# One-pass gate product, operands fetched ahead, and a re-ordered recurrence in a GLA + RWKV-7 block

## The chip, the cores and the metric

One Trainium2 chip, of which the kernel uses one core. The metric is the device time of one execution in microseconds (us), as the median of several runs. TensorE (PE) multiplies matrices from SBUF into PSUM; VectorE (DVE), ScalarE (ACT) and GpSimd (POOL) work on elements; SyncE (SP) issues the DMAs. Each engine runs its own instruction list in order and waits on semaphores that others raise.

## The reference, cut to what matters

x has 2048 rows of 1024. A row-normalised h = RMSNorm(x) is multiplied by a wide matrix; the columns feed a GLA branch, an RWKV-7 branch and two gates.

```python
p = h @ w_in                                     # GLA | RWKV-7 | merge gates
# GLA: chunked gated linear attention, forward and backward, 4 heads
la_f = log_sigmoid(af @ wa2_f + ba_f) / 16       # the gate product: af has 16 columns
la_b = log_sigmoid(ab @ wa2_b + ba_b) / 16
y_a  = (norm(gla(q, k, v, la_f) + flip(gla(flip ..., la_b))) * silu(og)) @ gla_proj
# RWKV-7: s = token shift of p; decay and a from low-rank products
w = decay(w0 + tanh(wl) @ w2); a = sigmoid(a0 + al @ a2); g = sigmoid(gl) @ g2
S_t = S_{t-1} diag(w_t) + (S_{t-1} a_t) b_t^T + v_t k_t^T;  y_t = S_t r_t   # both directions, 8 heads
y_b = (groupnorm(y) + sum(r * k * r_k) * v) * g @ rwkv_proj
x = x + (sigmoid(gA) * y_a + sigmoid(gB) * y_b) @ w_out
x = x + convglu(rmsnorm(x)); out = rmsnorm(x)
```

## The kernel before, in words

Large products are made of three passes: each operand is split into hi (rounded to float32r) and lo (the rest), and hi·hi, hi·lo and lo·hi are summed in one PSUM bank (`mm3`, L237). The stages, with their times in the profiled execution:

* **0 to 275 us**: RMSNorm, the v columns, the low-rank columns af (L393 to L406: PSUM rows 0 to 31 hold the product with the weights' hi, rows 32 to 63 that with their lo; both go to DRAM scratch d_af) and the first projections.
* **275 to 620 us, GLA**: `gla()` is a generator that is stepped beside the projections (`Weave`, L590). For each of 4 heads and 4 blocks of 512 tokens, `gla_gate` (L486) multiplies wa2 (64 rows, float32) with af into z, from which the decays follow.
* **620 to 1045 us, RWKV preparation**: `rwkv_prep(p, b)` (L725) for 4 head pairs and 4 blocks, beside the remaining projections. It loads twal (tanh of wl, and al), shifts k, r and v, makes three low-rank products from twal (L741, L747), the scans, the operands arbk that go to d_lt, the transposes of v (L799), and the bonus product from sr (L805, L807). Each `yield` hands over to the projections.
* **1045 to 1893 us, recurrence**: 32 chunks of 64 steps, both directions d side by side. For a chunk, `sc_mm` (L864) loads the operands Lt and makes the score blocks psc, seven chunks ahead (LA); `sc_ev` (L877) masks them on DVE into Q (L880) and in place (L881), then ACT copies parts of Q into Nb (L887) and the rest over Lt (L889). Every four chunks `invert` (L917) turns Nb into the triangular inverses TT. The chain from chunk to chunk is W (L990), U (L1014), S (L1025) and X (L1027); py and Y are the output.
* In the same loop `fill()` (L1127) spreads the gate projections (kind g, 36 units of 6 steps) and the GLA output projection (kind y, 32 units of 3 steps) over the chunks, two steps of four products at four places of a chunk. Its helpers `w_get` (load a weight into the single buffer wraw), `w_put` (split it into whi and wlo, two buffers each), `o_get`, `o_put`, `g_get` and `g_sig` are laid on fixed steps (L1164 to L1202): a weight is put two steps before its first use, and the next is fetched right after. All its loads and stores go through SP, and the operands, gates and results share three buffers ev.
* **From 1893 us** the merge, the output projection and the MLP, not touched.

Order: up to the recurrence a planner orders each engine's list by a simulated timeline and priorities. Inside the loop over chunks (L1283) the lists of PE, ACT, DVE and POOL stand in the order of the program (`manual_schedule`); SP's is still the planner's. PSUM and SBUF tiles rotate over the number of buffers that `bufs` gives, and a new tile waits for the last reader of the one that it replaces.

Of the kernel before, what the change touches and what calls it, by code (L numbers as in the profile page):

```python
# [23 lines left out]
NB = 4  # L24
# [80 lines left out]
def _pack(inputs):  # L105
# [9 lines left out]
    wa = np.zeros((64, 4, 128), np.float32)  # L115
    f, b = one("gla_wa2_f"), one("gla_wa2_b")
    for h in range(4):
        for r0 in (0, 32):
            wa[r0:r0 + 16, h, :64] = f[:, h * 64:h * 64 + 64]
            wa[r0 + 16:r0 + 32, h, 64:] = b[:, h * 64:h * 64 + 64]  # L120
# [46 lines left out]
def _body(tc, A, out, dump=None, upto=99):  # L167
# [12 lines left out]
    def scratch(name, shape):  # L180
        return dr.tile(shape, F32, name=name, tag=name)
# [3 lines left out]
    d_af = scratch("d_af", [64, T])  # L185
# [213 lines left out]
    for b in range(NB):  # L399
# [4 lines left out]
        o = ev.tile([128, 512], F32, name="ev", tag="ev")  # L404
        nc.scalar.copy(out=o[0:64, :], in_=ps[0:64, :])
        sync.dma_start(out=d_af[:, b * BT:(b + 1) * BT], in_=o[0:64, :])  # L406
# [17 lines left out]
    wa2 = gp.tile([64, 4, 128], F32, name="wa2")  # L424
    sync.dma_start(out=wa2, in_=A["wa2"])
# [43 lines left out]
    def gla_load(hs, b):  # L469
# [5 lines left out]
        af = gp.tile([64, 512], F32, name="af", tag="af", bufs=1)  # L475
        sync.dma_start(out=af, in_=d_af[:, ts])
# [247 lines left out]

    def rwkv_prep(p, b):  # L725
# [3 lines left out]
        twal = R["rp"].tile([128, 512], F32, name="twal", tag="twal")  # L729
        sync.dma_start(out=twal, in_=d_twal[:, ts])  # L730
# [3 lines left out]
        if b == 0:  # L734
            R["lora"] = R["rp"].tile([128, 2, 128], F32, name="lora", tag="lora")
            sync.dma_start(out=R["lora"], in_=A["lora"][:, :, pc])
# [17 lines left out]
        yield  # L754

# [39 lines left out]
        nc.scalar.copy(out=tmp, in_=sv[:, ::-1])  # L795
        for d, sx in enumerate((sv, tmp)):
# [8 lines left out]
        nc.vector.scalar_tensor_tensor(out=sr, in0=sr, scalar=vc("rk", p), in1=kp, op0=ALU.mult, op1=ALU.mult)  # L805
# [39 lines left out]
    NL = 2 * LA + 1  # L845
# [12 lines left out]
    qs = {}  # L858
# [5 lines left out]
    def sc_mm(s, d):  # L864
        Lt = cl.tile([128, 2, 4, 128], F32, name="Lt", tag="Lt", bufs=NL)
        sync.dma_start(out=Lt, in_=d_lt[d, :, chunk_of(s, d)])
        Q = cl.tile([128, 4, 128], F32, name="Q", tag="Q", bufs=NL)
# [9 lines left out]
    def sc_ev(c):  # L877
# [39 lines left out]
    def invert(n):  # L917
        X = cp.tile([128, 32, 32], F32, name="XX", tag="XX", bufs=2)
# [364 lines left out]
    with tc.manual_schedule(engines=ORDERED):  # L1283
        for s in range(32):
# [4 lines left out]
            if not last:  # L1289
                scale_bj(s + 1, 1, bjs[1])  # L1290
# [544 lines left out]
```

## Time and profile before

| | |
|---|---|
| time, median of 3 runs | 3528.93 us (3526.49 to 3532.44) |
| profiled execution: time, span | 3531.8 us, 3530.0 us |
| mean granted TensorE clock (share of 2.4 GHz) | 0.961 |
| PE / PE weight loads busy | 93% / 74% |
| DVE / ACT / POOL busy | 65% / 46% / 25% |
| DMA | 531 MB, 151 GB/s on the mean |

The span runs from the first to the last instruction. A group of rows further down is one view of the trace: busy time by stretch, waits by who waited for whom, or instructions in order of time. "A <- B" in a wait means that A's engine stood idle until B had ended. Matmuls are pipelined: the step from one to the next is the start of the next less its own start, shorter than its duration.

### The profile page before, as it was taken

How to read it: one execution, taken by the hardware profiler on the slowest of the kernel's cores; microseconds unless marked ns; L12 is line 12 of the kernel's file. 1: busy time of each engine (PE TensorE's matmuls, PEld its weight loads, DVE VectorE, ACT ScalarE, POOL GpSimd, SP SyncE). 2: the span in 40 equal slices, each digit the busy share in tenths (PEclk: the TensorE clock that was granted, in tenths of full speed). 3: DMA queues.
4: the chain of work that ended last, by engine and by line, in shares of the span. 5: the costliest groups of instructions: out<-in, count | busy, mean ns of one | idle time of the engine just before them, and what ended most of it. 6: DMA issues, size and time to landing. Idle time of an engine off the chain costs nothing.

```text
span 3530.0 us, 58016 instructions
## 1 busy us (share of the span) xinstructions
PE 3282.4 (93%) x22232; PEld 2626.9 (74%) x22232; DVE 2281.4 (65%) x3903; ACT 1609.0 (46%) x2912; POOL 875.7 (25%) x715
## 2 busy tenths in 40 slices
PE   7999999999988888887777999999999999999999
PEld 6787778766656777766666788888877888878887
DVE  5207664587865666666776566888989989623222
ACT  4214443455545776776644333544454444411111
POOL 1122222134440000000002411666665555000000
PEclk9999999999999998998888999999999999999999
DMA  4233343687875455556788846422242222523222
GB/s 150 94 117 108 127 141 122 187 227 224 232 214 180 150 183 157 171 184 195 229 254 282 294 142 191 134 81 89 79 136 96 84 84 78 182 82 112 80 85 63
DMA packets 403222, 531.29 MB, mean 151 GB/s; under 512 B 61504, under 2 KB 250560, under 8 KB 402944
## 3 DMA queue, kind: packets, MB, share of 16 engines
q1 hardware_dynamic: 402944, 527.58, 48.0%
q8 instruction: 175, 2.87, 0.3%
q14 instruction: 103, 0.84, 0.1%
HBM read 345.02 MB, written 181.93 MB: 149 GB/s over the span
## 4 chain that ended last, share of the span: by engine, by line
PE 48%; DVE 12%; DMA 6%; ACT 4%; issue 2%; SPq 1%; POOL 0%; DVEq 0%; ACTq 0%; POOLq 0%
PE pu L1638 20%; PE pg L241 6%; PE pd L1722 4%; PE pd L1724 4%; PE pd L1723 4%; PE pf L1218 3%; DVE tm L924 1%; DVE XX L925 1%; DMA d_m<-ev 1%; DMA wraw<-win 1%; DVE X L1027 1%; DVE gX L1004 1%; DVE wlo L227 1%; ACT TT L938 1%; DMA ev<-d_gate 1%
## 5 line engine op out<-in xcount | busy, mean ns | idle before, releaser
L227 POOL TENSOR_TENSOR wlo<-wraw,whi 128x1024 fp32r<-128x1024 f32 x46 | 115.3, 2507 | 1175.0 <-ACT whi L226 929.1
L1561 POOL TENSOR_TENSOR rw<-rw 128x512 f32<-128x512 f32 x168 | 282.1, 1694 | 72.4 <-DVE s3l L227 59.7
L1722 PE MATMUL pd<-wdh,whi 128*128 128x512 f32 x672 | 261.6, 391 | 0.9 <-DVE ug L1506 0.9
L1723 PE MATMUL pd<-wdl,whi 128*128 128x512 f32 x672 | 261.4, 389 | 0.0
L1724 PE MATMUL pd<-wdh,wlo 128*128 128x512 f32 x672 | 259.3, 389 | 0.0
L1218 PE MATMUL pf<-fop,whi 128*128 128x512 f32 x576 | 178.6, 448 | 85.3 <-ACT whi L226 58.3
L241 PE MATMUL pg<-hlo,whi 128*128 128x512 f32 x928 | 254.2, 407 | 0.0
L241 PE MATMUL pg<-hhi,whi 128*128 128x512 f32 x928 | 249.7, 404 | 3.1 <-ACT whi L226 3.1
L241 PE MATMUL pg<-hhi,wlo 128*128 128x512 f32 x928 | 248.2, 402 | 0.0
L241 PEld LDWEIGHTS pg<-hhi,whi 128*128 128x128 f32 x928 | 176.2, 192 | 55.9 <-issue 15.8
L241 PEld LDWEIGHTS pg<-hlo,whi 128*128 128x128 f32 x928 | 176.9, 194 | 53.9 <-issue 18.1
L241 PEld LDWEIGHTS pg<-hhi,wlo 128*128 128x128 f32 x928 | 176.1, 192 | 50.6 <-issue 14.3
L1218 PEld LDWEIGHTS pf<-fop,whi 128*128 128x128 f32 x576 | 114.1, 209 | 122.1 <-ACT whi L226 64.1
L226 ACT CAST whi<-wraw 128x1024 fp32r<-128x1024 f32 x114 | 119.5, 1048 | 112.9 <-PE pg L241 54.1
L1606 DVE SCALAR_TENSOR_TENSOR cv<-ug,vec,cv 128x511 f32<-128x511 f32 (+1 forms) x88 | 124.1, 1410 | 57.4 <-ACT cv L1605 57.4
L1711 ACT CAST whi<-wraw 128x1024 fp32r<-128x1024 f32 (+1 forms) x36 | 35.3, 980 | 267.1 <-PE pd L1723 186.6
L1722 PEld LDWEIGHTS pd<-wdh,whi 128*128 128x128 f32 x672 | 126.1, 188 | 29.9 <-issue 4.2
L1724 PEld LDWEIGHTS pd<-wdh,wlo 128*128 128x128 f32 x672 | 126.1, 188 | 26.2
L1723 PEld LDWEIGHTS pd<-wdl,whi 128*128 128x128 f32 x672 | 126.1, 188 | 25.7
L1613 ACT ACTIVATE cv<-cv 128x511 f32<-128x511 f32 (+1 forms) x84 | 53.3, 634 | 197.0 <-DVE cv L1607 197.0
L1714 DVE TENSOR_TENSOR wlo<-wraw,whi 128x1024 fp32r<-128x1024 f32 (+1 forms) x36 | 39.3, 1091 | 151.4 <-ACT whi L1711 151.4
L227 DVE TENSOR_TENSOR wlo<-wraw,whi 128x1024 fp32r<-128x1024 f32 x68 | 84.1, 1237 | 79.3 <-ACT whi L226 79.2
(482 smaller groups left out, 8119.9 us busy)
## 6 DMA issues: line engine op xcount, KB each, us to landing
rw<-wup SPq DMA_DIRECT2D x84, 512.0 KB, 3.5
wraw<-win SPq DMA_DIRECT2D x74, 512.0 KB, 4.3
Lt<-d_lt SPq DMA_DIRECT2D x64, 512.0 KB, 5.2
d_lt<-arbk SPq DMA_DIRECT2D x96, 256.0 KB, 3.9
d_gate<-ev SPq DMA_DIRECT2D x64, 256.0 KB, 3.7
X<-d_vt SPq DMA_DIRECT2D x64, 256.0 KB, 4.4
bj<-d_lt SPq DMA_DIRECT2D x128, 128.0 KB, 3.8
d_m<-ev SPq DMA_DIRECT2D x64, 256.0 KB, 5.3
```

The lines of the kernel that those rows point to most:

```text
L226: (hi_eng or nc.scalar.copy)(out=hi, in_=src)
L227: (lo_eng or nc.vector).tensor_tensor(out=lo, in0=src, in1=hi.bitcast(F32), op=ALU.subtract)
L241: nc.tensor.matmul(ps, (wh, wh, wl)[ph], (xh, xl, xh)[ph], start=(ph == 0 and i == 0), stop=(ph == 2 and i == n - 1))
L1218: nc.tensor.matmul(ps, (wh, wh, wl)[ph][:, k0 + k, :], (hi, lo, hi)[ph][:, k, :], start=i == first[u] and k == 0, stop=i == last[u] and k ...
L1561: ps_ = lambda o, x, y, op: nc.gpsimd.tensor_tensor(out=o, in0=x, in1=y, op=op)
L1606: nc.vector.scalar_tensor_tensor(out=c, in0=u[:, c0 - 1:c0 - 1 + n], scalar=vc("cw0", m), in1=c, op0=ALU.mult, op1=ALU.add)
L1613: nc.scalar.activation(out=g, in_=g, func=AF.Silu)
L1638: nc.tensor.matmul(ps, w_, x_, start=first and n == 0, stop=n == len(mm) - 1, skip_group_check=True)
L1714: nc.vector.tensor_tensor(out=al[:, 0:m], in0=raw[:, 0:m], in1=ah[:, 0:m].bitcast(F32), op=ALU.subtract)
L1722: nc.tensor.matmul(ps, a, wdh[k][:, cs], start=(k == 0), stop=False)
L1723: nc.tensor.matmul(ps, a, wdl[k][:, cs], start=False, stop=False)
L1724: nc.tensor.matmul(ps, l, wdh[k][:, cs], start=False, stop=False)
```

## The change

* *Gate product.* d_af gets 128 rows: hi and lo of the first product, hi of the second, and hi of the first again. wa2 gets 128 rows of float32r, hi in rows 0 to 95 and lo in rows 96 to 127. One float32r product per block and head takes the place of the float32 one.
* *Preparation.* `get_low` loads twal (and at the start of a head pair the low-rank weights) right after the three products of the block before. sr is scaled by r_k and k before the transposes of v, not after.
* *Scores.* The two directions' Q share one tile, with 8 buffers in place of 15 single ones; Lt has 14 buffers (15 before). `sc_ev` is cut in two: `sc_v` (the DVE part) stays, `sc_a` (the ACT part) comes later: that of direction 0 before the scores of direction 1, that of direction 1 in the next chunk behind scale_bj, unless an inversion starts. The copies into Nb take both directions at once.
* *Fill.* A weight is put five steps ahead of its first use, the first one already before the prologue; all loads and stores of the fill are issued by GpSimd.

```diff
-    wa = np.zeros((64, 4, 128), np.float32)
+    wa = np.zeros((128, 4, 128), np.float32)
-        for r0 in (0, 32):
+        for r0 in (0, 32, 64, 96):
...
-        o = ev.tile([128, 512], F32, name="ev", tag="ev")
+        o = ev.tile([128, 512], F32R, name="ev", tag="ev")
+        ol = ev.tile([128, 512], F32R, name="ev", tag="ev")
         nc.scalar.copy(out=o[0:64, :], in_=ps[0:64, :])
-        sync.dma_start(out=d_af[:, b * BT:(b + 1) * BT], in_=o[0:64, :])
+        nc.vector.tensor_tensor(out=ol[0:32, :], in0=ps[0:32, :], in1=o[0:32, :].bitcast(F32), op=ALU.subtract)
+        for r0, src in ((0, o[0:32]), (32, ol[0:32]), (64, o[32:64]), (96, o[0:32])):
+            sync.dma_start(out=d_af[r0:r0 + 32, b * BT:(b + 1) * BT], in_=src.bitcast(F32))
...
-    wa2 = gp.tile([64, 4, 128], F32, name="wa2")
-    sync.dma_start(out=wa2, in_=A["wa2"])
+    wa2 = gp.tile([128, 4, 128], F32R, name="wa2")
+    war = ev.tile([128, 4, 128], F32, name="ev", tag="ev")
+    sync.dma_start(out=war, in_=A["wa2"])
+    nc.scalar.copy(out=wa2, in_=war)
+    nc.vector.tensor_tensor(out=wa2[96:128], in0=war[96:128], in1=wa2[96:128].bitcast(F32), op=ALU.subtract)
...
-        af = gp.tile([64, 512], F32, name="af", tag="af", bufs=1)
+        af = gp.tile([128, 512], F32R, name="af", tag="af", bufs=1)
...
+    def get_low(p, b):
+        R["twal"] = R["rp"].tile([128, 512], F32, name="twal", tag="twal")
+        sync.dma_start(out=R["twal"], in_=d_twal[:, b * BT:(b + 1) * BT])
+        if b == 0:
+            R["lora"] = R["rp"].tile([128, 2, 128], F32, name="lora", tag="lora")
+            sync.dma_start(out=R["lora"], in_=A["lora"][:, :, p * 128:p * 128 + 128])
...
-        twal = R["rp"].tile([128, 512], F32, name="twal", tag="twal")
-        sync.dma_start(out=twal, in_=d_twal[:, ts])
+        if (p, b) == (0, 0):
+            get_low(0, 0)
+        twal = R["twal"]
...
         act_tail[0] = last
         yield
+        if (p, b) != (3, NB - 1):
+            get_low(p + (b + 1) // NB, (b + 1) % NB)
...
         nc.scalar.copy(out=tmp, in_=sv[:, ::-1])
+        nc.vector.scalar_tensor_tensor(out=sr, in0=sr, scalar=vc("rk", p), in1=kp, op0=ALU.mult, op1=ALU.mult)
         for d, sx in enumerate((sv, tmp)):
...
         yield
-        nc.vector.scalar_tensor_tensor(out=sr, in0=sr, scalar=vc("rk", p), in1=kp, op0=ALU.mult, op1=ALU.mult)
         pn = R["rs"].tile([128, 512], F32, name="pn", tag="pn", bufs=2)
...
-    NL = 2 * LA + 1
+    NL = 2 * LA
...
-        Q = cl.tile([128, 4, 128], F32, name="Q", tag="Q", bufs=NL)
+        if d == 0:
+            qg[s] = cl.tile([128, 2, 4, 128], F32, name="Q", tag="Q", bufs=LA + 1)
+        Q = qg[s][:, d]
...
-    def sc_ev(c):
+    def sc_v(c):
         s, d, Lt, Q, ps = c
         mb_ = mk[d].unsqueeze(1).to_broadcast([128, 4, 128])
         nc.vector.tensor_tensor(out=Q, in0=ps[0], in1=mb_, op=ALU.mult)
         nc.vector.tensor_tensor(out=ps[1], in0=ps[1], in1=mb_, op=ALU.mult)
-        if d == 0 and s % 4 == 0:
-            nbs[s // 4] = cp.tile([128, 8, 4, 32], F32, name="Nb", tag="Nb")
-        for q in range(4):
-            rr = slice(q * 32, q * 32 + 32)
-            c0 = (q % 2) * 32
-            nc.scalar.copy(out=nbs[s // 4][rr, (s % 4) * 2 + d], in_=Q[rr, :, c0:c0 + 32])
+
+    def sc_a(c):
+        if c is None:
+            return
+        s, d, Lt, Q, ps = c
+        if d:
+            if s % 4 == 0:
+                nbs[s // 4] = cp.tile([128, 8, 4, 32], F32, name="Nb", tag="Nb")
+            for q in range(4):
+                rr = slice(q * 32, q * 32 + 32)
+                c0 = (q % 2) * 32
+                nc.scalar.copy(out=nbs[s // 4][rr, (s % 4) * 2:(s % 4) * 2 + 2], in_=qg[s][rr, :, :, c0:c0 + 32])
         for e in range(2):
             nc.scalar.copy(out=Lt[EV[e], 1 - e], in_=ps[1][EV[e]])
...
             raw = wp.tile([128, 1024], F32, name="wraw", tag="wraw", bufs=1)
-            sync.dma_start(out=raw, in_=A["win"][units[u][1]] if units[u][0] == "g" else A["wpa"][units[u][1] // 2])
+            nc.gpsimd.dma_start(out=raw, in_=A["win"][units[u][1]] if units[u][0] == "g" else A["wpa"][units[u][1] // 2])
...
-        puts = [max(first[u] - 2, done_[wid[fresh[i - 2]]] + 1 if i > 1 else 0) for i, u in enumerate(fresh)]
+        puts = [max(first[u] - 5, done_[wid[fresh[i - 2]]] + 1 if i > 1 else 0) for i, u in enumerate(fresh)]
         for i, u in enumerate(fresh):
             if i:
                 at(puts[i - 1], w_get, u)
-            at(puts[i], w_put, u)
+                at(puts[i], w_put, u)
...
         w_get(0)
+        w_put(0)
         yield
...
+    fil(1)
     load_x(0)
...
         for s in range(32):
...
             if not last:
                 scale_bj(s + 1, 1, bjs[1])
+            sc_a(c1)
...
+            c0 = c1 = None
             if la < 32:
-                c = sc_mm(la, 0)
-                sc_ev(c)
+                c0 = sc_mm(la, 0)
+                sc_v(c0)
...
+            sc_a(c0)
             if la < 32:
-                c = sc_mm(la, 1)
-                sc_ev(c)
+                c1 = sc_mm(la, 1)
+                sc_v(c1)
             if fresh:
+                sc_a(c1)
+                c1 = None
                 sl.add(invert(s // 4 + 1))
```

The four other DMAs of the fill (o_get, g_get, and the stores of d_gate and d_m) change from `sync` to `nc.gpsimd` like w_get's; in the prologue sc_a follows sc_v at once; gn_out takes one Q pair for its two tiles.

## Rows read from the trace of the kernel before

**Rows 1.** The page's busy time by engine: us, share of the span, instructions.

```profile
PE 3282.4 (93%) x22232; PEld 2626.9 (74%) x22232; DVE 2281.4 (65%) x3903; ACT 1609.0 (46%) x2912; POOL 875.7 (25%) x715
```

**Rows 2.** Busy time by stretch; the columns are named in the first line.

```profile
core 0: us, PE busy (x) PEld busy (x) DVE busy (x) ACT busy (x) POOL busy (x), PEclk, DMA share, GB/s
275.00:620.00 345.00, 343.40 (x1819) 272.28 (x1819) 224.34 (x575) 146.01 (x353) 83.46 (x69) 1.00 0.40 127
620.00:1045.00 425.00, 393.49 (x1496) 277.55 (x1495) 325.96 (x420) 232.37 (x353) 164.85 (x116) 0.94 0.76 215
1045.00:1165.00 120.00, 96.87 (x1112) 77.58 (x1113) 58.60 (x113) 66.37 (x145) 5.74 (x9) 0.89 0.58 178
1165.00:1690.00 525.00, 445.34 (x7926) 367.93 (x7925) 345.88 (x660) 370.00 (x804) 0.00 (x0) 0.92 0.57 177
1690.00:1893.00 203.00, 148.43 (x1742) 118.71 (x1734) 158.84 (x336) 106.82 (x225) 2.46 (x1) 0.83 0.82 235
```

**Rows 3.** Waits of PE, 1165 to 1690: us in total, times, longest.

```profile
PE pf L1218 <- ACT whi L226: 44.0, 11, 6.7
PE pf L1218 <- ACT fop L226: 11.9, 3, 6.2
```

**Rows 4.** Waits of ACT, same stretch.

```profile
ACT Nb L887 <- DVE Q L880: 77.0, 46, 5.4
```

**Rows 5.** Waits of SP's queue, same stretch.

```profile
SPq L1154 <- DVE wlo L227: 43.3, 10, 7.8
```

**Rows 6.** Instructions in time, PE, 277 to 281: start, us, what.

```profile
278.10 1.12 PE L491 MATMUL z<-af,wa 64*128 64x512 f32 x2
279.15 1.19 PE L241 MATMUL pg<-hhi,whi 128*128 128x512 f32 x4
```

**Rows 7.** Waits of PE, 620 to 1045.

```profile
PE pw L741 <- DMA twal<-d_twal: 17.9, 9, 3.2
PE pn L807 <- DVE sr L805: 5.0, 6, 1.2
```

**Rows 8.** Waits of PE, 1045 to 1165.

```profile
PE pf L1218 <- ACT whi L226: 12.9, 3, 8.8
```

**Rows 9.** Groups by line, ACT, 1045 to 1893: busy us, mean ns, idle.

```profile
L887 ACT COPY Nb<-Q 32x128 f32<-32x128 f32 x256 | 75.6, 295 | 80.2 <-DVE Q L880 77.8
```

**Rows 10.** Busy time by stretch: an undisturbed chunk, and 24 chunks.

```profile
1236.50:1252.30 15.80, 15.80 (x265) 13.29 (x264) 7.46 (x12) 9.93 (x24) 0.00 (x0) 1.00 0.60 185
1173.10:1699.30 526.20, 444.93 (x7875) 367.15 (x7874) 346.80 (x665) 369.99 (x803) 0.00 (x0) 0.92 0.57 178
```

**Rows 11.** Instructions in time, 1235.9 to 1243.

```profile
1236.62 0.34 SPq L1154 DMA_DIRECT2D wraw<-win  x1
...
1237.50 1.10 PE L997 MATMUL py<-X,Lt 128*64 128x64 f32 x32
...
1238.17 0.86 SPq L866 DMA_DIRECT2D Lt<-d_lt  x2
...
1241.89 0.33 PE L874 MATMUL psc<-Lt 64*64 64x128 f32 x2
```

**Rows 12.** The page's DMA issues: count, KB each, median us to landing.

```profile
rw<-wup SPq DMA_DIRECT2D x84, 512.0 KB, 3.5
...
Lt<-d_lt SPq DMA_DIRECT2D x64, 512.0 KB, 5.2
...
d_m<-ev SPq DMA_DIRECT2D x64, 256.0 KB, 5.3
```

**Rows 13.** Waits of PE, 1690 to 1893.

```profile
PE pf L1218 <- ACT whi L226: 24.0, 5, 10.0
```

**Rows 14.** Chain that ended last by line, 1690 to 1893.

```profile
by line: DMA d_m<-ev 15.5%; DMA ev<-d_gate 10.3%; PE pf L1218 7.6%; issue 5.0%; DVE ev L1226 3.9%; DVE X L1027 3.3%; DMA d_y<-ys 3.1%; DVE gX L1004 3.1%; DVE mu L1060 3.0%; DMA bj<-d_lt 2.8%; DMA ev<-d_oa 2.6%; DVE Lt L1057 2.4%; DVE tm L92
```

**Rows 15.** Instructions in time, DVE, 868 to 910.

```profile
900.29 0.68 DVE L783 TENSOR_TENSOR arbk<-sr,cx 128x512 f32<-128x512 f32 x1
901.08 1.47 DVE L805 SCALAR_TENSOR_TENSOR sr<-sr,vec,kp 128x512 f32<-128x512 f32 x1
```

More of the change, by code (lines that the diff above doesn't have):

```diff
@@ L178, in _body, with scratch @@
     dr = pool(base, "dr", space=DRAM)
-    def scratch(name, shape):
-        return dr.tile(shape, F32, name=name, tag=name)
+    def scratch(name, shape, dt=F32):
+        return dr.tile(shape, dt, name=name, tag=name)
     d_gla = scratch("d_gla", [8, 128, T])
     d_vg = scratch("d_vg", [T, 512])
-    d_af = scratch("d_af", [64, T])
+    d_af = scratch("d_af", [128, T])
     d_rw = scratch("d_rw", [14, 128, T])
@@ L474, in gla_load @@
         ts = slice(b * BT, (b + 1) * BT)
-        af = gp.tile([64, 512], F32, name="af", tag="af", bufs=1)
-        sync.dma_start(out=af, in_=d_af[:, ts])
+        af = gp.tile([128, 512], F32R, name="af", tag="af", bufs=1)
+        sync.dma_start(out=af.bitcast(F32), in_=d_af[:, ts])
         q2 = gp.tile([128, 512], F32, name="q2", tag="q2", bufs=2)
@@ L733, in rwkv_prep @@
         sv = shifted(4 + 3 * p, b, "sv")
-        if b == 0:
-            R["lora"] = R["rp"].tile([128, 2, 128], F32, name="lora", tag="lora")
-            sync.dma_start(out=R["lora"], in_=A["lora"][:, :, pc])
         sg = []
@@ L857, in _body @@
         nc.gpsimd.memset(t[96:128, :, :, 0:32], 0.0)
-    qs = {}
+    qs, qg = {}, {}
     EV = (slice(0, 64), slice(64, 128))
@@ L917, in invert @@
     def invert(n):
+        nb = nbs.pop(n)
         X = cp.tile([128, 32, 32], F32, name="XX", tag="XX", bufs=2)
-        nc.vector.transpose(X.rearrange("p j i -> p i j"), nbs.pop(n).rearrange("p s b i -> p i s b"))
+        nc.vector.transpose(X.rearrange("p j i -> p i j"), nb.rearrange("p s b i -> p i s b"))
         yield
@@ L1039, in gn_out @@
     def gn_out(i):
+        gp_ = cl.tile([128, 2, 4, 128], F32, name="Q", tag="Q", bufs=LA + 1)
         tiles = (7 - i, 8 + i)
@@ L1046, in gn_out @@
                 sync.dma_start(out=y[:, d], in_=d_y[c0:c0 + 2, :, d].rearrange("c p f -> p c f"))
-            g = cl.tile([128, 4, 128], F32, name="Q", tag="Q", bufs=NL)
+            g = gp_[:, tt // 8]
             sync.dma_start(out=g, in_=d_g[:, tt * 128:tt * 128 + 128].rearrange("(a p) t -> p a t", p=128))
@@ L1176, in o_get @@
             fr[i] = ev.tile([128, 512], F32, name="ev", tag="ev")
-            sync.dma_start(out=fr[i], in_=d_h[b, 4 * h + i] if k == "g" else d_oa[i, :, b * BT:(b + 1) * BT])
+            nc.gpsimd.dma_start(out=fr[i], in_=d_h[b, 4 * h + i] if k == "g" else d_oa[i, :, b * BT:(b + 1) * BT])
         def o_put(k, b, h, i):
@@ L1193, in g_get @@
             gts[u] = ev.tile([128, 512], F32, name="ev", tag="ev")
-            sync.dma_start(out=gts[u], in_=d_gate[2 * units[u][1], :, units[u][2] * BT:(units[u][2] + 1) * BT])
+            nc.gpsimd.dma_start(out=gts[u], in_=d_gate[2 * units[u][1], :, units[u][2] * BT:(units[u][2] + 1) * BT])
         def g_sig(u):
@@ L1222, in fill @@
                     nc.scalar.copy(out=o, in_=ps)
-                    sync.dma_start(out=d_gate[m - 22, :, ts], in_=o)
+                    nc.gpsimd.dma_start(out=d_gate[m - 22, :, ts], in_=o)
                 else:
@@ L1226, in fill @@
                     nc.vector.tensor_tensor(out=gt, in0=ps, in1=gt, op=ALU.mult)
-                    sync.dma_start(out=d_m[m, :, ts], in_=gt)
+                    nc.gpsimd.dma_start(out=d_m[m, :, ts], in_=gt)
             yield
@@ L1246, in _body @@
             c = sc_mm(s, d)
-            sc_ev(c)
+            sc_v(c)
+            sc_a(c)
             fil(P1)
@@ L1255, in _body @@
             c = sc_mm(s, d)
-            sc_ev(c)
+            sc_v(c)
+            sc_a(c)
             for _ in range(6):
@@ L1303, in _body @@
             bg(1)
+            c0 = c1 = None
             if la < 32:
-                c = sc_mm(la, 0)
-                sc_ev(c)
+                c0 = sc_mm(la, 0)
+                sc_v(c0)
             bg(1)
@@ L1321, in _body @@
                 scale_bj(s + 2, 0, bjs[0])
+            sc_a(c0)
             if la < 32:
-                c = sc_mm(la, 1)
-                sc_ev(c)
+                c1 = sc_mm(la, 1)
+                sc_v(c1)
             if fresh:
+                sc_a(c1)
+                c1 = None
                 sl.add(invert(s // 4 + 1))
```

## The prediction

> **What bounds the kernel now.** I read the page's busy line first: TensorE (PE) is busy 93% of the span and no other engine is above 74% [rows 1]. PE is therefore the clock of the whole program, and only the places where it waits, or does needless work, are worth anything. The table by stage says where those are [rows 2]. In the GLA stage (275 to 620 us) PE is idle 345 − 343.4 = 1.6 us: there only less PE work helps. In the RWKV preparation (620 to 1045) it is idle 31.5 us, in the prologue of the recurrence (1045 to 1165) 23.1 us, in the recurrence while scores are still computed ahead (1165 to 1690) 79.7 us, in its tail (1690 to 1893) 54.6 us. The granted clock falls with them: 1.00 in the GLA stage, where PE never pauses, 0.94, 0.89, 0.92 and 0.83 after it, a mixture of the 2.4 and the 1.2 GHz level. What the change does not touch (before 275 and after 1893) I leave as it is.
>
> Then the waits of PE inside a stage. In the recurrence the fill product waits for the cast of its weights, 44.0 us in 11 waits, and for its operand halves, 11.9 us [rows 3]. Why is a cast of about 1 us late? The same view for ScalarE (ACT): it stands 77.0 us in front of the copies into Nb until VectorE (DVE) has masked the scores [rows 4]. ACT runs in program order, so the cast queued behind stands too. And SyncE (SP), which issues every DMA in order, stands 43.3 us in front of the fill's weight load until wlo is written [rows 5], with the loads of the recurrence behind it.
>
> **The change part by part**, in time of the profiled execution.
>
> *Gate product, 16 times.* Before: two passes, 278.10 to 279.15, that is 1.05 us from start to next start; the four single passes behind it take 1.19 us, their pipeline's fill included, 0.30 each at most [rows 6]. Saved 16 × (1.05 − 0.30) = 12.0 us, on an engine with no idle time. Added: per block one DVE subtraction, three more stores on SP and a second ev buffer at the projection of af, and twice the bytes per load of af. They lie beside PE-bound projections; if all four subtractions and stores came out they would cost a few us once. I take 12, between 9 and 13.
>
> *Preparation.* PE waits 17.9 us for twal and 5.0 us for sr [rows 7]. The twal load moves from the head of a block to just behind the previous block's three products, nearly a block earlier, and sr is scaled before the transposes. Both waits go: 22.9 us. What the moves cost: the twal load now waits on SP for those products, and the loads and stores queued behind it on SP wait as well; the DVE scaling may stand for GpSimd's arbk, with the v part behind it. Of the stage, (1 − 0.94) × 2 × 425 = 51 us run at 1.2 GHz, and at most 31.5 of them are idle, so at least 19.5 us of work runs at half speed and loses 9.8 us. Fewer pauses give some of that back, say 8. What is late next is DVE (326 of 425 us busy) and the DMA engines (0.76) [rows 2]; for that I subtract 6. Gain 25, between 12 and 35.
>
> *Prologue.* The first weights are fetched and cast before load_x, later ones five steps ahead, not two. PE's three waits for them are 12.9 us [rows 8]. The weight buffer is single, and the score loads compete for the DMA engines, so I take 11, between 5 and 20.
>
> *Recurrence, weights and ACT's order.* With a put five steps ahead, at two steps a visit, the cast has two visits of slack, and in between ACT no longer stands before the masked scores, since those copies now come a visit later. The 44.0 us go. The Nb copies become half as many and twice as long: one takes 295 ns [rows 9], the new one between 295 and 590, so ACT wins between 38 and 0 us; not counted, since ACT is not the bound. The waits for the operand halves hang on DMAs that SP issued late; on GpSimd's queue, idle here (POOL 0.00), I count half, 6. From the clock, (1 − 0.92) × 2 × 525 = 84 us at the lower level, against 79.7 idle: 2 us of loss at least, 42 at most; I take 8, nearer to the low end because many of the lower stretches hold the waits themselves.
>
> The Trainium skill speaks against this part: "DMA: Bandwidth & Descriptors", section "Issuing engines are not separate DMA queues", says that starting DMAs from more engines saves only the sequencer's time. By that rule the 6 us would fall away and the sum be 6 us longer. The trace agrees in so far as what is to be saved is a sequencer's: SP's standing time is of that kind.
>
> *Recurrence, what comes late instead.* A buffer of Lt is taken away (15 to 14). With 15, the first load of a chunk was released in the chunk before. With 14 it needs the buffer that the py products of this chunk still read. In an undisturbed chunk py runs from 1237.50, a load so released is issued at 1238.17, and the score product of the first direction, which will need such a load, starts at 1241.89 [rows 11], 3.7 us later. Over all loads of Lt the median landing is 5.2 us; loads of the same 512 KB in the MLP land in 3.5 [rows 12]. So the price in each of some 24 chunks is between 0 and 5.2 − 3.7 = 1.5 us; I take 0.5, as this load stands first of its pair on SP: 12 us. And X is copied behind the delayed sc_a on ACT: 0.25 us a chunk, 6 us. Together 44 + 6 + 8 − 12 − 6 = 40, between 10 and 65.
>
> That this isn't more than the chunk can give: a chunk that waits for nothing takes 15.8 us with PE busy throughout, the 24 chunks from 1173.1 on take 526.2/24 = 21.9 [rows 10].
>
> *Tail.* PE waits 24.0 us for weights [rows 13]. But here the chain is largely the ring of three ev buffers: store of d_m 15.5%, load of the gate 10.3% of the stretch [rows 14], and DVE is busy 158.8 of 203 us. The ring stays, its DMAs now on another queue whose issue no row shows. Below, SP's own weight issue is 0.34 us [rows 11]; above, a whole landing, 5.3 us [rows 12]. I take about 1, nearer to the issue row. Gain 10, between 0 and 22.
>
> **Sum**: 12 + 25 + 11 + 40 + 10 = 98 us. The profiled execution took 3531.8 us (span 3530.0, 1.8 around it), 2.9 over the median of 3528.93. So 3433.8 for such an execution, **3431 us** as a median. All low ends together (9, 12, 5, 10, 0) are 36 us, 3493; all high ends (13, 35, 20, 65, 22) are 155 us, 3374.
>
> **The rivals.**
>
> *The look-ahead load becomes the new wait.* If each first Lt load lands 5.2 us after its release, 24 × 1.5 = 36 us instead of 12 are lost, and PE's pauses keep the clock gain of 8 away: 32 us more, 3463. For it: the median of all loads of Lt. Against: the 3.5 us of loads of that size where there is less traffic, and a queue that the fill's DMAs have left. Chance 0.15.
>
> *GpSimd's issues hold VectorE up.* POOL did nothing in the recurrence so far. Where it works, a DVE operation takes 1.47 us, and without it 0.68 [rows 15]. The fill has 184 DMAs (52 weights, 32 operand loads, 32 gate loads, 68 stores, counted from its lists); were one DVE operation behind each lengthened by 0.79 us, that is 145 us of DVE, of which I put a quarter on PE's path: 36 us, 3467. Against: many DVE operations here read PSUM. Chance 0.08.
>
> The Trainium skill names the reverse: "SBUF — State Buffer", section "SBUF: two separate sides", says that a DVE copy in a two-port mode keeps GpSimd from writing descriptors, so that a transfer from its queue waits. Nearly all DVE work here is of two operands, not copies; by that rule the fill's DMAs would be late, and the time lie near this rival's.
>
> *The chunks fall to what PE needs.* 15.8 us and some 2.6 for the inversion's products and small waits, 18.4 × 24 = 442, gain 84 instead of 40: 3387. For it: the undisturbed chunks. Against: ACT's 370 us of work must fit into the shorter time in order. Chance 0.12.
>
> *Slower: the fill's queue becomes the bound.* From 1045 to 1893 there are 848/184 = 4.6 us per DMA of the fill. POOL takes them in order, and a gate load stands until an earlier store has landed. If every one stood for a landing of 5.3 us, the phase would last 975 us, 127 more; less 37 won earlier, 90 us slower than before: 3619. It decides from (848 + 37)/184 = 4.8 us each. Against: only loads that reuse a buffer just stored should wait. Chance 0.05.
>
> **How the numbers follow.** Forecast 0.60, the rivals 0.15, 0.08, 0.12 and 0.05. The range that should hold 8 in 10 is 3374 to 3493, the ends of the sum, and takes in the first three rivals. Within 0.2% (7 us, what a measurement of this kernel can just tell) lies almost nothing: 0.02, the slow side of the queue rivals. Slower 0.04, faster 0.94.
>
> **What would show it.** Products z of 0.3 us; no PE wait for twal or sr; the stage table 12, 25, 11, 40 and 10 us shorter, with clocks nearer to 1.00; no ACT wait at Nb for Q; PE waits for whi in the recurrence below 10 us. A new PE wait of the scores for Lt, more than 0.5 us a chunk, would speak for the first rival, longer DVE rows beside POOL for the second, PE waits for whi that trace back to a late weight DMA for the last. The prediction is wrong if the early stages keep their length, or if chunks stay near 21.9 us.

## The result: slower, and the profile after

The changed kernel takes 3556.07 us (median of 4 runs, 3550.28 to 3562.70) against 3528.73 for the kernel before on the same chip: ratio 1.0083, 95% interval 1.0068 to 1.0097. It is slower by 27 us, where I had forecast 98 us of gain. The profiled execution took 3553.29 us, its span is 3551.5.

The busy line of the page after [rows 1] says little: PE 93% of the span, its weight loads 74%, DVE 64%, ACT 45%, POOL 28%.

The table by stage of the kernel after (columns as in [rows 2]). The borders move with the work, so that each stretch holds what its counterpart in [rows 2] holds; the last score product, at 1690.2 before and 1711.4 after, ends the recurrence proper.

```profile
275.00:608.00 333.00, 331.70 (x1828) 275.12 (x1827) 226.74 (x574) 146.49 (x354) 84.90 (x70) 1.00 0.44 137
608.00:1038.00 430.00, 395.17 (x1498) 277.74 (x1496) 322.97 (x422) 235.87 (x359) 169.68 (x121) 0.93 0.78 216
1038.00:1152.00 114.00, 93.12 (x1086) 75.72 (x1088) 60.05 (x112) 57.15 (x106) 12.53 (x23) 0.84 0.58 177
1152.00:1711.20 559.20, 463.98 (x7928) 381.40 (x7932) 346.11 (x662) 350.09 (x709) 56.56 (x105) 0.88 0.55 167
1711.20:1907.00 195.80, 141.47 (x1738) 114.92 (x1730) 158.44 (x338) 106.84 (x225) 36.08 (x60) 0.84 0.86 243
```

Read the lengths against [rows 2]: 345 to 333, 425 to 430, 120 to 114, 525 to 559, 203 to 196. So −12, +5, −6, +34, −7, and 7.5 more from there to the end (1637.0 to 1644.5): +21.5, the difference of the two spans. The gate product did what it should; the preparation gained nothing; the recurrence lost 34 us instead of gaining 40, at a lower granted clock (0.88 against 0.92). Of these 34, PE's own busy time is 18.6 (445.3 to 464.0 for as many products) and its idle time 15.6 (79.7 to 95.2). Of the last 7.5 us, 5.9 lie in the merge, which the change does not touch: from its first product to the first of the output projection it took 104.0 us before and 109.9 after.

PE's waits in the recurrence after [rows 3]:

```profile
PE pu L1038 <- ACT W L1016: 21.1, 4, 6.2
PE pz L977 <- ACT bkt L936: 18.9, 6, 3.3
PE pf L1244 <- ACT fop L226: 16.6, 9, 3.2
PE pf L1244 <- ACT whi L226: 15.5, 6, 5.8
PE psc L890 <- DMA Lt<-d_lt: 8.8, 8, 2.8
```

whi, the cast of a weight, fell from 44.0 to 15.5 us; the forecast had it below 10. In its place PE waits for W and for bkt (the transposed operands of the next state), which are ScalarE's copies too, longer than before for fop (the operand halves of the fill), and a little for Lt. The waits of ScalarE itself, same stretch [rows 4]: Nb no longer waits for Q; instead

```profile
ACT TT L962 <- DVE XC L956: 31.7, 12, 6.1
```

What that means is seen in one chunk in which an inversion ends (chunk 3). Instructions of ScalarE in time, kernel after:

```profile
1188.99 1.17 ACT L912 COPY Lt<-psc 64x512 f32<-64x512 f32 x2
1196.25 2.50 ACT L962 COPY TT<-XC 32x512 f32<-32x512 f32 x4 [6.09 <-DVE XC L956]
1199.88 1.25 ACT L962 COPY TT<-XC 32x512 f32<-32x512 f32 x2 [1.12 <-DVE XC L956]
...
1201.63 0.59 ACT L1016 COPY W<-pw 128x512 f32<-128x512 f32 x1
...
1203.44 1.63 ACT L910 COPY Nb<-Q 32x256 f32<-32x256 f32 x4
1205.08 1.17 ACT L912 COPY Lt<-psc 64x512 f32<-64x512 f32 x2
1206.27 1.24 ACT L962 COPY TT<-XC 32x512 f32<-32x512 f32 x2
1207.53 1.05 ACT L226 CAST whi<-wraw 128x1024 fp32r<-128x1024 f32 x1
1208.60 0.59 ACT L936 COPY bkt<-ptr 128x512 f32<-128x512 f32 x1
1209.09 0.58 ACT L1040 COPY X<-pu 64x512 f32<-64x512 f32 x1
```

And the same chunk in the kernel before:

```profile
1207.64 1.22 ACT L887 COPY Nb<-Q 32x128 f32<-32x128 f32 x4 [0.43 <-DVE Q L880]
1208.87 1.18 ACT L889 COPY Lt<-psc 64x512 f32<-64x512 f32 x2
1210.32 2.50 ACT L938 COPY TT<-XC 32x512 f32<-32x512 f32 x4 [0.28 <-DVE XC L932]
1213.94 1.25 ACT L938 COPY TT<-XC 32x512 f32<-32x512 f32 x2 [1.12 <-DVE XC L932]
1215.21 1.04 ACT L226 CAST whi<-wraw 128x1024 fp32r<-128x1024 f32 x1
1216.28 0.59 ACT L992 COPY W<-pw 128x512 f32<-128x512 f32 x1
```

Before, the six evictions of the last scores (four copies into Nb, two over Lt, 2.4 us) ran while the inversion's transpose XC was on its way: they cost nothing. After, ScalarE idles there for 6.09 us, and the evictions, 2.8 us, come behind W, with bkt and X queued behind them. X belongs to the chain from chunk to chunk. And the cast of whi before: its weights had long landed (no ScalarE wait in that stretch names that load); it stood behind the TT copies, like W right behind it.

### The profile page after: what moved, and what is told of

Its sections match the earlier page's. It is cut to its first block, busy times and chain, and to the rows that moved or that the text cites. A ratio compares the mean times of both kernels' runs of the same rounds, so it can differ in the third digit from the quotient of the medians.

```text
span 3551.5 us, 57952 instructions
## 1 busy us (share of the span) xinstructions
PE 3285.3 (93%) x22216; PEld 2639.7 (74%) x22216; DVE 2281.5 (64%) x3908; ACT 1586.2 (45%) x2785; POOL 977.1 (28%) x899
## 4 chain that ended last, share of the span: by engine, by line
PE 50%; DMA 11%; DVE 9%; issue 7%; ACT 3%; POOL 2%; SPq 1%; DVEq 0%; POOLq 0%; ACTq 0%
PE pu L1673 20%; PE pg L241 8%; PE pd L1757 4%; PE pd L1759 4%; PE pd L1758 4%; PE pf L1244 2%; DMA d_lt<-arbk 1%; DMA Lt<-d_lt 1%; DMA twal<-d_twal 1%; DMA wraw<-win 1%; PE pw L753 1%; DMA bj<-d_lt 1%; DMA d_m<-ev 1%; ACT TT L962 1%; DVE tm L948 1%
## 5 line engine op out<-in xcount | busy, mean ns | idle before, releaser
L1244 PE MATMUL pf<-fop,whi 128*128 128x512 f32 x576 | 183.8, 456 | 50.0 <-ACT fop L226 16.6
L241 PEld LDWEIGHTS pg<-hhi,wlo 128*128 128x128 f32 x928 | 176.1, 192 | 48.5 <-issue 10.7
L1759 PEld LDWEIGHTS pd<-wdh,wlo 128*128 128x128 f32 x672 | 126.1, 188 | 26.2
```

What stands on the lines that cost most here:

```text
L241: nc.tensor.matmul(ps, (wh, wh, wl)[ph], (xh, xl, xh)[ph], start=(ph == 0 and i == 0), stop=(ph == 2 and i == n - 1))
L1244: nc.tensor.matmul(ps, (wh, wh, wl)[ph][:, k0 + k, :], (hi, lo, hi)[ph][:, k, :], start=i == first[u] and k == 0, stop=i == last[u] and k ...
L1759: nc.tensor.matmul(ps, l, wdh[k][:, cs], start=False, stop=False)
```

## The experiments

Each kernel was timed in five rounds beside the kernel before; ratios are to that, whose median was between 3527.5 and 3531.5 in every set, so that medians of two sets can be set side by side to about 4 us. A chunk's length is counted from its first W product to that of the next; "first to last pS" is the stretch between the state products (pS) of the first and the last chunk that has them. Theory A: ScalarE's order, the deferred evictions. B: GpSimd's queue. C or W: when weights are cast. O: it is only the order of ScalarE's queue that makes whi, W or X late. L: the layout of device memory.

**e1, the early parts alone** (gate product, preparation).

> The kernel before with the one-pass gate product and the preparation's edits alone; scores, recurrence and fill as before. All theories agree that this part is no loss by itself; they differ in the preparation. In the changed kernel the last gate product stood 11.0 us earlier than before (516.7 against 527.7), the recurrent stage ended 9.4 earlier, and the preparation then took 410 us against 405. If the preparation's edits themselves cost these 5 us: 3530 - 10 + 5 = about 3524, with the preparation again some 410 us long. If the 5 us came from what follows or from chance phases of the weight loads: 405 us, and about 3519. If they gained the 25 us that I forecast: 3494.

3535.69 us, ratio 1.0020 (1.0010 to 1.0031): slower than before, which none of the three cases had. Its preparation began 12.9 us earlier than before and ended 2.9 earlier. Something was at work that I had not thought of.

**e2, evictions in line.**

```diff
-            sc_a(c1)                # behind W of the next chunk
...
                 sc_v(c0)
+                sc_a(c0)
...
-            sc_a(c0)
...
                 sc_v(c1)
+                sc_a(c1)
```

> The changed kernel with the evictions sc_a(c0) and sc_a(c1) put back right behind sc_v, nothing deferred; shared score tile, 14 look-ahead buffers, weights 5 steps ahead and GpSimd's queue stay. Theory A, ScalarE's order: in the chunks where the inversion ends (3, 7, 11, 15, 19, 23) the deferred evictions, 2.8 us of ScalarE, stand between the W copy and the bkt and X copies, while ScalarE idles ahead of the XC transposes; these six chunks grew by 5.8 + 6.0 + 1.2 + 5.5 + 3.7 - 0.2 = 22 us. Undone, 15 to 22 us come back: 3532 to 3540, the waits pu<-W and pz<-bkt (40 us) fall to about 20. Theory B, GpSimd's queue, and theory C, weights too far ahead: these waits are not set by the deferral, 3548 to 3560.

3531.54 us, ratio 1.0008 (0.9996 to 1.0020): 24.5 us better than the changed kernel. Theory A holds in the time: the chunks 3, 7, 11, 15, 19 and 23 are 28.7 us shorter together. But of the two waits that it named only that for bkt went (18.9 to 3.1), while that for W rose from 31.9 to 38.8. PE's waits from the first to the last pS in e2:

```profile
PE pu L1038 <- ACT W L1016: 38.8, 9, 7.9
PE pf L1244 <- ACT whi L226: 20.3, 6, 5.3
```

Most of the gain is not idle time. The same stretch as busy time (columns as in [rows 2]), after and in e2:

```profile
1150.80:1855.00 704.20, 573.78 (x9428) 471.42 (x9428) 458.02 (x895) 433.79 (x885) 80.75 (x150) 0.87 0.62 185
1150.70:1826.80 676.10, 556.63 (x9427) 457.16 (x9428) 458.25 (x893) 433.98 (x884) 80.00 (x149) 0.90 0.64 192
```

Of the 28.1 us between the two, 17.2 are PE's busy time for the same products, at a granted clock (a mixture of the 1.2 and 2.4 GHz levels) of 0.87 after and 0.90 in e2, and 10.9 are idle time.

**e3, the fill on SP's queue again** (the five `nc.gpsimd.dma_start` of fill back to `sync`).

> The changed kernel with the fill's loads and stores (weights, operands, gates, results) back on SP's queue; all else as changed. Theory B, GpSimd's queue: the operand loads stand in order behind a weight load that waits for its buffer, and land 6 us after issue; chunks 6 and 18 grew by 5.4 + 5.9, the way from the end of preparation to the first score by 7, the merge by 10. On SP these 28 us mostly come back: 3525 to 3535. Theory A, ScalarE's order: at most the 11 us of chunks 6 and 18, 3543 to 3553, and chunks 3, 7, 11, 15, 19 keep their 32 to 35 and 26 to 29 us.

3549.39 us, ratio 1.0054 (1.0041 to 1.0067): 7 us better, not 28. Chunks 6 and 18 fell from 34.5 and 34.4 us to 27.9 each; chunks 3, 11, 15 and 23 kept theirs. B is not the main cause. But GpSimd's queue has a price: the fill's operand loads land 6.3 us behind their issue in the changed kernel and 3.7 in e3 (medians of 32), and PE's waits for these operands, those for DVE's part included, fall from 23.3 to 14.7 us. Against that, its waits for Lt grow from 8.8 to 19.0.

**e4, weights two steps ahead** (`first[u] - 5` to `- 2`).

> The changed kernel with the fill's weights cast 2 steps ahead of use instead of 5. Theory C, weights too far ahead: casts now fall between the recurrence's own copies on ScalarE (in chunk 3 a 1.05 us cast ahead of bkt) and put weight loads ahead of the operand loads on the queue; at 2 the loss of chunks 3, 6, 15 and 18 (22 us together) goes, 3530 to 3540. Theories A and B: the wait of the fill for whi, which fell from 44.0 to 15.5 us in the recurrence, comes back by 15 to 28, and the long chunks stay: 3565 to 3585.

3550.77 us, ratio 1.0066 (1.0053 to 1.0080). C falls, and so does what A and B had to say: casting earlier or later makes hardly a difference here (5 us by the medians, and the two intervals overlap).

**e5, the other way round: before, with weights five steps ahead** (`first[u] - 2` to `- 5`).

> The kernel before with one edit: the fill's weights are cast 5 steps ahead of their use instead of 2. Theory W, as my prediction had it: PE's 44 us of waits for whi in the recurrence are weights cast too late; cast earlier, they go, and 25 to 44 us are gained, 3485 to 3505. Theory O, ScalarE's order: ScalarE never waited for a weight's load there, the cast only stood in the queue with the copies of the recurrence behind Nb<-Q and TT<-XC; moved ahead, the same 1.05 us stand before W, bkt or X, and PE waits for these instead: whi falls, pu<-W and pz<-bkt rise by as much, 3520 to 3535.

3522.71 us, ratio 0.9974 (0.9962 to 0.9985): 8 us of gain, at O's end. PE's waits, first to last pS:

```profile
PE pu L1014 <- ACT W L992: 20.2, 9, 4.9
PE pf L1218 <- DVE ev L1226: 19.4, 8, 5.0
PE pf L1218 <- ACT fop L226: 19.1, 3, 7.1
PE pf L1218 <- ACT whi L226: 12.8, 3, 4.5
```

Before, the same view has whi 64.7, fop 11.9, W 9.3, ev 8.4. whi gave up 52 us; the three others took 29 of them.

**e6, the gate product alone.**

> The kernel before with the one-pass gate product alone, without the preparation's edits. With both, the time was 3535.7 and the preparation took some 10 us longer (its start 12.9 us earlier than before, its end 2.9). If the preparation's edits cost that: the gate product alone keeps its 11 us to the end, 3516 to 3520. If the preparation only gives back what an earlier start brings (transfers fall together otherwise): 3526 to 3536, and its stretch is as long as with the edits.

3538.82 us, ratio 1.0021 (1.0010 to 1.0033). So the preparation's edits are not to blame: the gate product's 12.8 us were there at the preparation's start and 1.7 were left at its end. The loads of twal there landed in 4.6 us in the median, against 4.1 before.

**e7, TT copies on GpSimd** (in invert, `nc.scalar.copy(out=tt...)` to `nc.gpsimd.tensor_copy`).

> The kernel before with one edit: the eight copies TT<-XC of each inversion (0.62 us each on ScalarE) run on GpSimd, which has nothing else in the recurrence. Theory O: in the chunks where an inversion ends (3, 7, 11, ...) ScalarE's queue stands behind the DVE transpose XC and then carries 5 us of TT copies ahead of W, of casts and of X; that goes, chunks 3, 11, 15 and 23 fall from 29 to 32 us to about 24 to 27, some 15 to 25 us in all with the prologue: 3505 to 3518. Theory W (late weights set these waits): below 5 us, 3524 to 3530. If copies on GpSimd are over 2 us each, pu waits for TT instead, and it is slower: 3535 to 3550.

3520.41 us, ratio 0.9974 (0.9963 to 0.9986): 10 us, less than O said. Chunks 3, 11, 15 and 23 fell to 25.5, 26.2, 25.6 and 26.4 us, 17.7 us together; chunks 24, 26 and 30, whose work waits for transfers, grew by 6.5. O names the wait rightly and does not see what takes it over.

**e8, e2 and e3 and e7 together.**

> The changed kernel with evictions in line (as e2), the fill's DMAs on SP (as e3) and the copies TT<-XC on GpSimd (as e7). Theory O: in e2 pu waited for W 6.4, 3.1, 6.4 and 7.9 us in chunks 3, 11, 15 and 23, behind the TT copies; with these on GpSimd 15 to 20 of the 24 us go, so 3508 to 3520. If only the deferral mattered and not who stands ahead of W: 3526 to 3533, as e2.

3544.99 us, ratio 1.0036 (1.0024 to 1.0049): a miss, 13 us worse than e2. Chunk 3 did fall (29.3 to 27.4), but the scores now waited for Lt in 14 of the chunks 1 to 24. e17 takes that up.

**e9, the layout alone.** The gate product's edit doubles d_af in device memory from 64 to 128 rows of 8 KB: 512 KB more, and every scratch tensor that the build places behind it moves by that. e9 is the kernel before with this and nothing else:

```diff
-    d_af = scratch("d_af", [64, T])
+    d_af = scratch("d_af", [128, T])      # stores and loads use d_af[0:64]
```

> The kernel before with one edit that changes no work: the scratch tensor d_af in device memory has 128 rows as in the changed kernel, of which only the old 64 are used, so that every scratch tensor allocated behind it (d_gla, d_h, d_rw, d_lt, d_gate and so on) lies 512 KB further. Theory L, layout: in all kernels with the gate product's edit the transfers of the preparation land later (twal, rw, lt and their like: 4.2 to 4.4 us on average against 3.9) and those late in the recurrence too (5.7 against 5.2); the layout alone does this, and costs 15 to 20 us against the gate product's own gain of 11: 3540 to 3550. Theory P, the plan: the planner's other order of projections and preparation gives the 11 us back, the layout does nothing: 3527 to 3533.

3548.92 us, ratio 1.0057 (1.0043 to 1.0070): 20 us slower, with the same instructions and the same bytes; the two profiled executions are 9.4 apart. The page's queue line (packets, MB, share of the DMA engines), before:

```profile
q1 hardware_dynamic: 402944, 527.58, 48.0%
```

and in e9:

```profile
q1 hardware_dynamic: 402944, 527.58, 49.0%
```

The loss is not in the preparation, which ended 4.9 us earlier than before, but mainly in the tail, from the last score product to the first product of the merge. Before, and in e9 (columns as in [rows 2]):

```profile
1690.20:1898.10 207.90, 148.22 (x1734) 118.51 (x1726) 162.53 (x344) 108.31 (x227) 4.80 (x2) 0.83 0.82 237
1685.70:1902.80 217.10, 149.98 (x1734) 119.56 (x1726) 162.57 (x344) 108.09 (x227) 4.80 (x2) 0.81 0.81 227
```

**e10, the gate product with the tensors 8 MB further** instead of 512 KB.

```diff
-    d_af = scratch("d_af", [128, T])
+    d_af = scratch("d_af", [1088, T])[0:128]
```

> The gate product's edit alone (as e6) with d_af made 1088 rows long, of which 128 are used: the scratch tensors behind it lie 8 MB further than in the kernel before instead of 512 KB. Theory L, if what counts is how the tensors' addresses stand within a power of two up to 8 MB: as in the kernel before again, the landings are back at 3.9 us in the preparation, and the gate product's 11 us stay to the end: 3517 to 3523. Theory P, or a layout whose cost does not come back at 8 MB: 3534 to 3542, as e6.

3518.38 us, ratio 0.9974 (0.9963 to 0.9985): 20 us better than e6, and the gate product's gain is there at the end (by the end of the preparation 6.1 of its 12.5 us are left here too; the rest comes back in the prologue). In the profiled executions, 21.2 us apart, 4.4 of these are there at the end of the preparation; the tail is 213.8 us in e10 against 220.7 in e6. The preparation's loads of twal land in 4.1 us in the median before, in 4.7 in e9 and 4.0 in e10. That is a sign of the layout, not the place of the loss: PE waits 22.5 us for them in e9 and 23.9 in e10.

**e11, only c1 in line.**

> The changed kernel with only the second direction's evictions sc_a(c1) back behind sc_v(c1); the first direction's sc_a(c0) stays deferred. Theory A says that the harm is done by c1's 2.8 us (four Nb and two Lt copies), which the change puts into the next chunk behind the W copy, ahead of bkt and X: nearly all of e2's gain of 24 us comes back, 3528 to 3537. If it is the deferral as such (c0's two Lt copies behind Y and bj as well): about half, 3538 to 3548.

3531.54 us, ratio 1.0012 (1.0000 to 1.0024), the same as e2: the whole harm of the deferral is c1's six copies behind W.

**e12, e5 and e7 together.**

> The kernel before with e5's and e7's edits together: weights cast 5 steps ahead and the TT copies on GpSimd. Theory O: e7 leaves waits for whi in chunks 6, 9, 12, 17, 21 and 24 (31 us together), which e5 mostly removed (9: 6.1 to 0, 21: 12.4 to 4), and e5's waits for W in chunks 3, 11 and 15 (11 us) lie behind the TT copies that e7 takes away; the two gains of 8 and 10 us add, or more: 3505 to 3514. If they are one and the same wait: 3517 to 3522.

3513.45 us, ratio 0.9963 (0.9948 to 0.9978): 15 us, close to the sum of 8 and 10, at the slow end of O's range: two waits, not one.

**e13, the changed kernel at the layout of e10.**

> The changed kernel with d_af 1088 rows long (128 used), so that the scratch tensors lie 8 MB instead of 512 KB further than before; all else as changed. Theory L and theory A together: the layout's part of the loss, 15 to 20 us as between e10 and e6, comes back, the deferral's 24 us stay: 3534 to 3541. If the layout matters only where SP's queue carries the fill (it was measured on the kernel before): 3548 to 3557.

3537.75 us, ratio 1.0033 (1.0022 to 1.0043): 18.3 us better than the changed kernel.

**e14, e2 at that layout.**

> e2 (evictions in line) at the layout of e13. If the two causes add, 3531 less 15 to 20: 3511 to 3517, which is the gate product's 11 us and a little from the rest of the change. If what remains of the change were worth the 98 us of my forecast: 3431 to 3450. If the layout's cost is already gone with the deferral: 3527 to 3533.

3513.41 us, ratio 0.9958 (0.9943 to 0.9972): 42.7 us better than the changed kernel, where 24.5 and 18.3 make 42.8. The two causes add, and with both out the change is a gain of 14 us, 10 of which the gate product has alone (e10).

**e15, e1 at that layout.**

> e1 (gate product and the preparation's edits on the kernel before) at the layout of e13; e10 is the same without the preparation's edits, 3518.4. The look-ahead load of twal still goes out 4 to 7 us ahead of its use, since it stands on SP's queue behind the stores of the block before, so the edits are worth little: 3514 to 3520. If the bad layout hid the 25 us of my forecast: 3493 to 3500.

3516.91 us, ratio 0.9971 (0.9961 to 0.9982), against 0.9974 of e10: the preparation's edits are worth nothing that can be measured.

PE's waits in e15 from the first to the last pS, with the old recurrence:

```profile
PE pf L1232 <- ACT whi L226: 69.0, 15, 10.0
PE pf L1232 <- ACT fop L226: 12.2, 3, 6.1
...
PE pu L1028 <- ACT W L1006: 10.4, 5, 4.9
PE pf L1232 <- DVE ev L1240: 7.8, 4, 3.1
```

and in e14, with the new one:

```profile
PE pu L1038 <- ACT W L1016: 39.9, 10, 7.3
PE pf L1244 <- ACT whi L226: 18.4, 6, 5.3
PE pf L1244 <- ACT fop L226: 13.3, 3, 5.6
PE pf L1244 <- DVE ev L1252: 11.9, 5, 4.5
...
PE psc L890 <- DMA Lt<-d_lt: 8.8, 5, 3.7
PE psc L890 <- DVE Q L896: 5.0, 3, 2.6
```

Here is where the forecast 44 us went: whi gives up 50.6 us, and W takes 29.5 of them, Lt 8.8, Q 5.0, ev (the fill's results) 4.1, fop 1.1, which makes 48.5.

**e16, what helped, together:** before with the gate product at e10's layout, weights five steps ahead, TT copies on GpSimd.

> The kernel before with the gate product at the layout of e10, the weights 5 steps ahead (e5) and the TT copies on GpSimd (e7). e10 gained 10 us, e12 (e5 and e7 together) 15; if they add: 3500 to 3506. If an earlier start is given back in the transfers of the late recurrence: 3509 to 3514.

3494.21 us, ratio 0.9910 (0.9895 to 0.9924): 33 us faster than before, more than the sum of 25.

**e17, e14 with the fill on SP.**

> e14 (changed kernel, evictions in line, good layout) with the fill's DMAs back on SP. Theory B, GpSimd's queue costs: the operand loads land sooner (chunks 6 and 18 were 32 us), and 5 to 10 us come back: 3503 to 3508. The other way: on SP the look-ahead loads Lt stand behind the fill's, with 14 buffers they are late, and psc waits for them 15 to 20 us instead of 8.8: 3519 to 3526. No difference: 3511 to 3516.

3540.41 us, ratio 1.0024 (1.0014 to 1.0033), 27 us slower than e14 by the medians, 23 by the ratios: GpSimd's queue is worth that much here, more than the cases had. The scores' wait for Lt, 8.8 us in e14, is now

```profile
PE psc L890 <- DMA Lt<-d_lt: 24.3, 12, 5.3
```

That accounts for 15.5 us. Another 12.4 is PE's busy time from the first to the last pS (554.6 us in e14, 567.0 here, for the same products at a lower granted clock, 0.91 and 0.89). Whether a fifteenth buffer of Lt would have caught the wait was not tried. Beside the deferral (e3) the same exchange went the other way by 7 us; why the balance tips there stays open.

**e18, e16 with the preparation's edits.**

> e16 (3494.2) with the preparation's edits added. e15 against e10 gave them 1.5 us, within what can be told apart: 3490 to 3497. If they matter once the transfers are less crowded: 3482 to 3488.

3492.04 us, ratio 0.9892 (0.9875 to 0.9909): the fastest kernel, 38 to 39 us below before, though its lead over e16 is within what can be told apart.

## Why the prediction was wrong, point by point

The account from the runs, starting at 3528.7: gate product −10.2 (e10), preparation −1.5 (e15 to e10), all of the new recurrence, prologue and tail with the evictions in line −3.5 (e14 to e15), the layout +18.3 (e13), the deferral +24.5 (e2). That makes 3556.3; 3556.07 was measured. The first three terms are steps of one path, so what the sum tests is that layout and deferral add; and the −1.5 and −3.5 are within what can be told apart.

*Gate product, 12 us: right.* The last product z stands 11.2 us earlier, the stage is 12 shorter. A product z after [rows 6]:

```profile
279.51 0.39 PE L498 MATMUL z<-af,wa 128*128 128x512 f32 x1
279.74 1.07 PE L241 MATMUL pg<-hhi,whi 128*128 128x512 f32 x4
```

The next product starts 0.23 us behind it. What I costed as "twice the bytes per load of af" had a price that I did not look for: the place of everything behind d_af. That term, +18 to +20, was put at nothing: it stood in no part of the sum and in no rival.

*Preparation, 25 us: wrong.* The step that failed is "The twal load moves from the head of a block to just behind the previous block's three products, nearly a block earlier". It moved in the text of the program; SP's order hardly changed. SP's queue in time, after:

```profile
969.74 1.34 SPq L800 DMA_DIRECT2D d_lt<-arbk  x2
971.18 0.95 SPq L804 DMA_DIRECT2D d_lt<-arbk  x1
972.23 1.63 SPq L734 DMA_DIRECT2D twal<-d_twal  x1
```

It still goes out behind the stores of the block before. This one, used at 979.18, is 7.0 us ahead of its use and in time; over the 16 loads the median is 5.4 us ahead, where it was 4.6 before, and a block takes some 25. Nine of the loads are still waited for, and PE waits no less than before [rows 7]:

```profile
PE pw L753 <- DMA twal<-d_twal: 23.5, 9, 3.7
```

I had named SP's queue and then let the load pass it. The wait for sr hardly moved either (5.0 to 4.1), and of the 25 us the runs show 1.5 (e15 against e10).

*Prologue, 11 us:* 13.5 from the first score to the first pS, of which 7 had been lost ahead of the first score, 6 in the stage's row. The sign is right by luck. From the last bonus product of the preparation to the first pS it is 120.0 us before and 113.4 after, but 110.3 in e15 and 111.3 in e6, which have the old prologue: PE's waits for whi there had fallen from 12.9 to 5.2 and 4.2 without the early weights. With the new one e14 takes 115.0: no run shows a gain from the early weights there.

*Recurrence, 40 us: wrong,* and the step that decided the forecast. "The 44.0 us go" is true of the row, and false of the time. The row names what PE's next instruction lacks, not what is short: the cast lay in ScalarE's queue beside W, bkt and X, and a cast moved up lets PE run on to the next of these (e5: 52 us of waits for whi less, 8 us of time; e14). The test was in the trace: in the stretch of [rows 4] ScalarE has no wait for a weight load. *"X is copied behind the delayed sc_a on ACT: 0.25 us a chunk, 6 us"* is the term that was mis-sized: I spread it over all chunks, it falls on the few in which the inversion ends, with W, bkt and X in line, and costs 24.5 us (e2, e11). The 8 us from the clock came with the other sign: the granted clock fell from 0.92 to 0.88, and PE's busy time rose by 18.6. So did the 6 us for the operand halves: their loads land 6.3 us behind issue on GpSimd's queue, 4.8 on SP's before, and PE's waits for fop from ScalarE rose from 11.9 to 16.6. Even with the evictions in line and at the good layout this part gains nothing: from the first pS to the last score product it is 526.6 us before, 523.7 in e15 with the old recurrence and 533.3 in e14 with the new one. The five steps alone make it 518.4 (e5), so the rest of the new recurrence, the 14 buffers, the shared tile of Q and GpSimd's queue, costs time there; which of them does was not taken apart.

*The tail, 10 us:* 7 measured, at the layout that makes a tail longer (e9). From the last score product to the merge's first it is 198.1 us in e14 and 213.8 in e15, so the new recurrence gains 15.7 there, the only stretch in which it does. The merge then gives back 5.8 of it (108.5 us in e14, 102.7 in e15), so that the output projection starts level in both (1985.6). Why the merge is longer stays open.

*The rivals.* "The look-ahead load becomes the new wait" is there and is small: 8.8 us, where I had put 12 into the sum; in e17 it grows to 24.3. "GpSimd's issues hold VectorE up" did not happen: the mask product onto Q takes 0.69 us before and after, and DVE is busy 345.9 and 346.1 us in the recurrence. The two rows behind its 0.79 us [rows 15] are of two different operations, so their difference was no measure of it. The fill's operand loads did land later on GpSimd's queue (6.3 us against 3.7 in e3); whether DVE's work has to do with it no run shows. "Slower: the fill's queue becomes the bound" had the sign and not the mechanism: with the fill back on SP the changed kernel is 7 us better (e3), at the good layout with the evictions in line 23 to 27 worse (e17). The Trainium skill's rule in "DMA: Bandwidth & Descriptors", section "Issuing engines are not separate DMA queues", is that other issuers save only the sequencer's time to start a transfer, usually small beside the transfer. The rows agree as far as starting goes: an issue of a fill weight takes 0.34 us on SP, its landing 4.3. What SP has besides in e17 is its standing in front of waits, 60.4 us for the fill's gate results alone (from the first to the last pS), with the loads of Lt behind it. How much of e17's loss is due to this was not separated.

## What to carry to other kernels

A wait of PE for an engine that works in order is a wait for its queue: ask what stands ahead of the late instruction and what comes right behind it before counting the wait as gain, and put work that nobody waits for into the stretch where that engine stands anyway. A load is as early as its place in the issuing queue, not as its line in the program. When a wait gets shorter or longer, compare PE's busy time for the same products too: here more than half of the deferral's loss was in it. When an edit makes a scratch tensor in device memory larger, time the kernel with that edit to the layout alone.

## What the runs showed of the hardware that I had not expected

Where scratch tensors lie in device memory is worth 20 us of 3529 (e9 against before; e10 against e6): moved by 512 KB the same loads of twal landed in 4.7 us in the median, moved by 8 MB in 4.0, unmoved in 4.1, and the tail grew by 9.2 us in e9. Which property of the address does it was not tried. The Trainium skill describes an effect of layout in "DMA: Bandwidth & Descriptors", section "Latency and other measured facts": rows at a pitch of a large power of two are slower, and a few KiB of padding cure it. No run here changed a pitch.

A copy of 32x512 elements takes 610 ns on GpSimd (median in e7) against 617 on ScalarE (mean, after), so the eight TT copies take no longer where GpSimd idles. A transfer started from GpSimd lands later behind its issue: the 52 weight loads of the fill 4.9 us in the median after, 4.3 with the same loads on SP (e3), the 32 operand loads 6.3 against 3.7.
